# High and low weight tiles of 1032 columns, the last eight unused

## The chip, the cores and the metric

The kernel runs on one core of a Trainium2 chip. The metric is the device time of one execution, in microseconds. Before the change it is 2703.74 us, the median of three runs (2702.44 to 2708.98).

## What is computed

A two-layer backbone over 512 latent tokens and 256 context tokens of width 1024. Each layer is a half-step SwiGLU, a mixing stage with three groups of heads, and another half-step SwiGLU; shift, scale and gate come from a conditioning vector. All of it is in float32.

```python
for l in range(DEPTH):                                   # DEPTH = 2
    ml = jnp.split(s_lat @ w_mod[l] + b_mod[l], 9, axis=-1)
    mc = jnp.split(s_ctx @ w_mod[l] + b_mod[l], 9, axis=-1)
    x = half_ffn(x, g_norm[l, 0], ml[0], ml[1], ml[2], w_gate[l, 0], w_up[l, 0], w_down[l, 0])
    ctx = half_ffn(ctx, g_norm[l, 0], mc[0], mc[1], mc[2], w_gate[l, 0], w_up[l, 0], w_down[l, 0])
    h_lat = modulate(rms_norm(x, g_norm[l, 1]), ml[3], ml[4])
    h_ctx = modulate(rms_norm(ctx, g_norm[l, 1]), mc[3], mc[4])
    y_l, y_c = token_mixing(h_lat, h_ctx, w_in[l], w_out[l], ...)
    x = x + ml[5] * y_l
    x = half_ffn(x, g_norm[l, 2], ml[6], ml[7], ml[8], w_gate[l, 1], w_up[l, 1], w_down[l, 1])
    ...
# half_ffn: h + 0.5 * gate * ((silu(m @ wg) * (m @ wu)) @ wd),  m = modulate(rms_norm(h), shift, scale)
```

`half_ffn` has 2816 hidden columns, in 22 blocks of 128. The mixing stage is grouped-query attention, a short gated convolution and multi-head latent attention on one input projection, with one output projection behind them.

## The kernel before

Activations lie transposed, features on the 128 partitions and tokens along the row: `xT[0..7]` hold the stream, 128x768 each. A matrix product in float32 is made of three products in float32r: every operand is kept as a high part (the value rounded to float32r) and a low part (the remainder), and `mm3` (line 284) issues weight-high times data-high, weight-high times data-low and weight-low times data-high into one accumulator. So each 128x128 block of weights costs three matmuls per stretch of tokens, two with the high tile of the weights and one with the low tile, and each matmul loads its weights anew. In `PE MATMUL ps<-s,wh` of a profile, `s` is the moving operand (activations) and `wh` the weights.

Weights come in blocks of 128 rows by 1024 columns, which is eight 128x128 blocks. `wload` (line 194) fetches one into a raw tile `wr`. `wsplit` (line 199) makes the two parts: ScalarE copies `wr` to the high tile `wh`, and VectorE subtracts `wh` from `wr` into the low tile `wl`. Tiles `wh` and `wl` come from a pool with three buffers for each tag, so six buffers in all that are handed out in turn. Lines 554 and 873 take tiles of the same two tags, for a third early block and in the feed-forward of the last layer. In the mixing stage the tags also serve query and key tiles (`qh`, `ql`, `k`, 768 columns). Raw weights also come from other tiles: `wu` (tag `mscr`), `ws` (sums of weights, tag `mr`), `t` (down projections).

Most feed-forward blocks use a scheme of seven products on quarter matrices in place of eight; it needs sums of weights (`Weights.sums`, line 754, and `Sums` in the last layer, line 879) which go through the same split.

The order on TensorE, VectorE and ScalarE is written out by hand in most stages (`chain` and `behind` add an order without a semaphore). DMAs for weights are issued on SP's queue; some that add onto a tile come from GpSimd's. All vector, scalar and matrix instructions are recorded through one helper, so all of them have line 67 in the profile; tiles tell them apart.

SBUF addresses are given out by tag, one tag behind the other in the pool, each tag's buffers side by side.

Of the kernel before, what the change touches and what calls it, by code (L numbers as in the profile page):

```python
# [9 lines left out]
F32R = mybir.dt.float32r  # L10
# [5 lines left out]
P = 128  # L16
# [32 lines left out]
def tile_net(ctx: ExitStack, tc: tile.TileContext, a, out):  # L49
# [37 lines left out]
    pool = ctx.enter_context(tc.tile_pool(name="pool", bufs=1))  # L87
# [4 lines left out]
    def nm(s):  # L92
        uid[0] += 1
        return f"{s}{uid[0]}"
# [13 lines left out]
    def po():  # L108
        return psum.tile([P, 512], F32, name=nm("po"), tag="po", bufs=4)

    def f32(t):
        return t.bitcast(F32)
# [78 lines left out]
                mod_block(*mod_queue.pop(0))  # L191


    def wload(src, w):
        raw = pool.tile([P, 1024], F32, name=nm("wr"), tag="wr", bufs=NWR)
        nc.sync.dma_start(out=raw[:, :w], in_=src)
        return raw

    def wsplit(raw, w, hi=None, lo=None, eng=None):
        if hi is None:  # L200
            hi = pool.tile([P, 1024], F32R, name=nm("wh"), tag="wh", bufs=3)
            lo = pool.tile([P, 1024], F32R, name=nm("wl"), tag="wl", bufs=3)
        se.copy(hi[:, :w], raw[:, :w])
        (eng or ve).tensor_sub(lo[:, :w], raw[:, :w], f32(hi)[:, :w])
        return hi, lo
# [21 lines left out]
    def wblock(src, w=1024):  # L227
        return wsplit(wload(src, w), w)
# [89 lines left out]
    def rsqrt(ms, n, tag="rs", bufs=3):  # L318
        y, steps = rsqrt_steps(ms, n, tag, bufs)
        for f in steps:  # L320
            f()
        return y
# [96 lines left out]
    def lat_mm(acc, wb, h, k, cols, view):  # L419
        c = slice(k * P, (k + 1) * P)  # L420
        mm3(wb[0][:, c], wb[1][:, c], h[k][0], h[k][1], packed(acc, cols, view), k == 0, k == KD - 1)

    def residual(blocks, rhs, gate, streams, nxt, pre=None, late={}, view=nv, npump=0, ntail=3):
# [30 lines left out]
        if not two:  # L454
            return None
        held = [(o, blocks(o)) for o in range(KD - ntail, KD)]
        raws = [wload(src, 1024) for src in pre[:2]]
        E = []
        nk = len(rhs)

        def second_block():
            E.append(wsplit(raws[1], 1024, *(pool.tile([P, 1024], F32R, name=nm("we"), tag=t, bufs=1)
                                             for t in ("mscr", "mq"))))
            raws.append(wload(pre[2], 1024))

        chain("te", "ve", "se")
        for n, (o, wb) in enumerate(held):
            pt = po()
            project(packed(pt, c0, view), wb, rhs)
            update(o, cv(pt, c0), c0, i0)  # L470
            if n:
                S[0].accumulate()
            S[0].square(tv(xT[o], c0))
            if n == 1:
                E.append(wsplit(raws[0], 1024, *(pool.tile([P, 1024], F32R, name=nm("we"), tag="mr", bufs=2)
                                                 for _ in range(2))))
            elif n == 3:
                second_block()
# [5 lines left out]
        def run(count):  # L484
            for _ in range(count):
                if not units:
                    return
                n, k = units.pop(0)
                if k == 0:
                    if n % 2 == 0:  # L490
                        tiles[n // 2] = ps()
                project(packed(tiles[n // 2][:, BANK * (n % 2):BANK * (n % 2 + 1)], c1, view), held[n][1], rhs, [k])
                if k == nk - 1:
                    ready.append(n)
# [3 lines left out]
        def second_update():  # L498
            if ready:
                n = ready.pop(0)  # L500
                o = held[n][0]
                update(o, cv(tiles[n // 2][:, BANK * (n % 2):BANK * (n % 2 + 1)], c1), c1, i1)
                updated.append(o)

        def second_square():

            if updated:
                n = squared[0]
                squared[0] += 1
                if n % 3 == 0:  # L510
                    squared[1] = temp()
                w = S[1].w
                sq = squared[1][:, n % 3 * w:n % 3 * w + w]
                se.activation(out=cv(sq, c1), in_=tv(xT[updated.pop(0)], c1), func=AF.Square)
                s1.append(sq)
# [27 lines left out]
        def products(k):  # L543
            for n in range(len(accs)):
                lat_mm(accs[n], E[n], h, k, c0, hview)

        third = []
        for k in range(KD + 1):
            if k < KD:
                cur = HMod(h[k], k, c0, R, A[i0][:, k:k + 1], B[i0][:, k:k + 1], hview)  # L550
                cur.scaled()
                cur.high()
            if k == 4 and len(E) == 2:
                third.extend(pool.tile([P, 1024], F32R, name=nm(t), tag=t, bufs=3) for t in ("wh", "wl"))
                se.copy(third[0], raws[2])
            if prev is not None:
                prev.low()
            if k == 5 and third:
                ve.tensor_sub(third[1], raws[2], f32(third[0]))
                E.append(tuple(third))  # L560
            second_update()
            second_square()
            run(3)
            if k == 1:
                S[1].zero()
                S[1].count(S[1].acc, False)
            if k >= 1:
                for _ in range(2 if k < 6 else len(s1)):
                    if s1:
                        S[1].count(s1.pop(0), not (s1 or ready or updated or units))  # L570
            if k == 6:
                S[1].mean()
                r1 = rsqrt(S[1].ms, S[1].w // P)
            if prev is not None and (k <= hold or k == KD):
                products(k - 1)
            prev = cur
            if k == 7:

                R1 = po()
                for j in range(S[1].w // P):  # L580
                    te.transpose(out=R1[:, j * P:(j + 1) * P], in_=r1[:, j:j + 1].to_broadcast([P, P]), identity=ident)
                if len(accs) == 2:
                    accs.append(po())
                    for kk in range(hold):
                        lat_mm(accs[2], E[2], h, kk, c0, hview)
                for kk in range(hold, 7):
                    products(kk)
# [17 lines left out]
    def ffn(l, f, hin, streams, nxt, pre, npump, late={}):  # L605
# [111 lines left out]
        for ci in range(nslow):  # L717
            m0, n = chunks[ci]
            acts, ahead = [], {}
            for m in range(m0, m0 + n):  # L720
                if i == 0 and m > 1:
                    pump(2 - ci)
                acts.append(classical(m, ahead))
                if i == 0 and m < 2:
                    pump(2)
                if m in sums_at:
                    if m + 1 < m0 + n:
                        for j in range(2):
                            if 2 * (m + 1) + j >= len(E):
                                ahead[m + 1, j] = wblock(a[("wg", "wu")[j]][i, m + 1])  # L730
                    sums(sums_at.index(m))
            if ci == 0:
                pump(upto=gate)
            residual(down(m0, n), acts, gate, streams, None, view=view)
# [55 lines left out]
        lo, hi = slice(0, hw), slice(hw, w)  # L790
# [74 lines left out]
        def narrow():  # L865
# [4 lines left out]
            W = {}  # L870

            def high_part(raw, n=1024):
                hi = pool.tile([P, 1024], F32R, name=nm("wh"), tag="wh", bufs=3)
                lo = pool.tile([P, 1024], F32R, name=nm("wl"), tag="wl", bufs=3)
                se.copy(hi[:, :n], raw[:, :n])
                return (hi, lo), lambda: ve.tensor_sub(lo[:, :n], raw[:, :n], f32(hi)[:, :n])

            class Sums:
# [27 lines left out]
                def split_gate(self):  # L906
                    self.w1, low = high_part(self.g)
                    return low

                def split_sums(self):  # L910
                    self.w2, low = high_part(self.s)
                    return low

                def split_up(self):
                    self.w3, low = high_part(self.u)
                    return low
# [35 lines left out]
            for ci in range(1, len(LAST)):  # L952
                m0, n = LAST[ci]
                tiles = []
                for m in range(m0, m0 + n):
# [8 lines left out]
                    if j == 0:  # L964
                        t = nt
# [20 lines left out]
                    t = Tile(m, W[m])  # L986
# [153 lines left out]
        for ci in range(nslow, len(chunks)):  # L1140
# [3 lines left out]
            for m in range(m0, m0 + n):  # L1144
                end = m == m0 + n - 1
                nx = None
                if m == m0:

                    t = nt
# [23 lines left out]
                t = Tile(m)  # L1173
# [275 lines left out]
    def mixing(l, hin, early, streams, nxt, pre):  # L1449
# [513 lines left out]
        pump(upto=(l, 7))  # L1963
        pump(upto=(l, 6))
        return residual(lambda o: first_out[0] if o == 0 else wblock(a["wo"][l, o]), rhs, (l, 5), streams, nxt, pre, npump=2)

    def cst(name, l, shape):
# [276 lines left out]
```

## Time and profile before

| | |
|---|---|
| median of three runs | 2703.74 us |
| the profiled execution: its time | 2708.69 us |
| its span, first to last instruction | 2706.8 us |
| granted TensorE clock | 0.998 |
| matmuls | 16,088, TensorE busy 98% of the span |
| VectorE / ScalarE / GpSimd busy | 76% / 42% / 5% |
| DMA | 266.09 MB, 98 GB/s over the span |

Matmuls are pipelined, and the profile models their ends. The busy time of TensorE is a union of overlapping spans, so a matmul of 384 columns shows some 334 ns although the next one starts 173 ns later. The distance between starts, from the timeline, is what a matmul costs. A row of the timeline merges like instructions that follow each other: its start, the time they cover, and their count. PEld is the weight load, which runs beside the matmul before it. A row of the groups ends with the idle time of the engine just before these instructions and what ended it.

### The profile page before, as it was taken

What the parts mean: (1) busy time and instruction counts of PE and PEld (TensorE: products, weight loads), DVE (VectorE), ACT (ScalarE), POOL (GpSimd) and SP (SyncE); (2) the same over time, 40 slices, a digit from 0 to 9 for tenths busy, and PEclk for the clock granted to TensorE, in tenths of its full rate; (3) what the DMA queues carried; (4) which work ended last, traced back from release to release, by engine and by line L of the source; (5) the groups of instructions that cost most, each with busy time, mean ns of one, the idle gap of its engine ahead of it and who ended that gap; (6) DMA issues with size and microseconds to landing.
All of it is one profiled execution on the core that took longest, in us unless ns stands there. A gap on an engine that the chain in (4) does not pass through costs nothing. (4 is left out here: it accounts for less than half of the span.)

```text
span 2706.8 us, 40646 instructions
## 1 busy us (share of the span) xinstructions
PE 2647.6 (98%) x16088; PEld 2513.8 (93%) x16088; DVE 2047.0 (76%) x3493; ACT 1140.6 (42%) x1991; POOL 147.3 (5%) x224
## 2 busy tenths in 40 slices
PE   8999999999999999999999999999999999999999
PEld 5999999989888889999999999999998888889988
DVE  6856777777789987777777777777767798676655
ACT  5223333341478633333334433333343488444433
POOL 0000000000230100000000000000000221001110
PEclk9999999999999999999999999999999999999999
DMA  7313333234100321333333123333325101246544
GB/s 253 117 59 106 105 105 108 84 88 149 36 2 9 110 94 55 108 103 109 109 109 102 59 83 106 109 104 104 101 88 162 49 9 40 92 126 176 148 134 120
DMA packets 102927, 266.09 MB, mean 98 GB/s; under 512 B 12240, under 2 KB 41680, under 8 KB 102736
## 3 DMA queue, kind: packets, MB, share of 16 engines
q1 hardware_dynamic: 96112, 249.33, 27.8%
q0 software_dynamic: 6624, 14.16, 2.6%
q8 instruction: 127, 2.08, 0.3%
q14 instruction: 64, 0.52, 0.1%
HBM read 256.63 MB, written 2.10 MB: 96 GB/s over the span
## 5 line engine op out<-in xcount | busy, mean ns | idle before, releaser
L67 PE MATMUL ps<-s,wh 128*128 128x384 f32 (+2 forms) x4292 | 983.6, 338 | 7.5 <-ACT t L67 3.8
L67 PEld LDWEIGHTS ps<-s,wh 128*128 128x128 f32 x4292 | 742.5, 188 | 51.3 <-issue 5.2
L67 PE MATMUL po<-s,wh 128*128 128x384 f32 (+2 forms) x3164 | 765.2, 327 | 2.9 <-ACT t L67 2.2
L67 PE MATMUL ps<-s,wl 128*128 128x384 f32 (+2 forms) x2146 | 610.4, 337 | 1.3 <-DVE wl L67 1.2
L67 PEld LDWEIGHTS po<-s,wh 128*128 128x128 f32 x3164 | 554.4, 189 | 15.5 <-ACT t L67 3.3
L67 PE MATMUL po<-s,wl 128*128 128x384 f32 (+2 forms) x1582 | 517.2, 327 | 0.0
L67 PEld LDWEIGHTS ps<-s,wl 128*128 128x128 f32 x2146 | 387.3, 188 | 20.1 <-DVE wl L67 3.5
L67 PEld LDWEIGHTS po<-s,wl 128*128 128x128 f32 x1582 | 299.1, 189 | 5.4
L67 DVE SCALAR_TENSOR_TENSOR junk<-mr,sb 128x1024 fp8e4<-128x1024 f32 x224 | 273.7, 1222 | 16.1 <-DMA mr<-in_wm_dram 15.3
L67 DVE TENSOR_TENSOR wl<-wr,wh 128x1024 fp32r<-128x1024 f32 (+3 forms) x179 | 193.1, 1081 | 112.9 <-ACT wh L67 112.7
L67 DVE SCALAR_TENSOR_TENSOR xT<-ps,mod,xT 128x256 f32<-128x256 f32 (+1 forms) x360 | 198.7, 594 | 103.4 <-PE ps L67 101.3
L67 ACT CAST wh<-wr 128x1024 fp32r<-128x1024 f32 (+3 forms) x179 | 165.2, 926 | 202.9 <-PE ps L67 137.7
L67 ACT COPY t<-po 128x384 f32<-128x384 f32 (+2 forms) x215 | 96.9, 451 | 258.9 <-PE po L67 258.5
L67 PE MATMUL po<-s,s 128*128 128x256 f32 (+3 forms) x1216 | 191.9, 309 | 7.3 <-ACT s L67 2.7
L67 PEld LDWEIGHTS po<-s,s 128*128 128x128 f32 x1216 | 173.8, 191 | 14.8 <-ACT s L67 3.4
L67 ACT ACTIVATE t<-t 128x384 f32<-128x384 f32 (+1 forms) x142 | 70.9, 499 | 255.0 <-DVE t L67 255.0
L67 DVE TENSOR_TENSOR t<-po,t 128x384 f32<-128x384 f32 (+2 forms) x223 | 115.7, 524 | 34.2 <-ACT t L67 23.9
L67 DVE TENSOR_TENSOR s<-t,s 128x768 fp32r<-128x768 f32 (+3 forms) x144 | 104.2, 727 | 43.4 <-ACT s L67 42.9
L67 ACT CAST wh<-ws 128x1024 fp32r<-128x1024 f32 x71 | 74.6, 1051 | 147.0 <-PE ps L67 90.6
L67 ACT CAST s<-t 128x768 fp32r<-128x768 f32 (+3 forms) x144 | 92.6, 649 | 102.7 <-DVE t L67 102.5
L67 PE MATMUL po<-s,w 128*128 128x384 f32 x636 | 118.7, 334 | 0.0
L67 ACT CAST wh<-t 128x768 fp32r<-128x768 f32 x80 | 66.7, 837 | 113.6 <-PE ps L67 108.7
(197 smaller groups left out, 3306.7 us busy)
## 6 DMA issues: line engine op xcount, KB each, us to landing
mr<-in_wm_dram SPq DMA_DIRECT2D x128, 512.0 KB, 3.3
wr<-in_wg_dram SPq DMA_DIRECT2D x82, 512.0 KB, 3.3
wu<-in_wu_dram SPq DMA_DIRECT2D x71, 512.0 KB, 3.3
t<-in_wd_dram SPq DMA_DIRECT2D x80, 384.0 KB, 3.6
wr<-in_wiT_dram SPq DMA_DIRECT2D x22, 512.0 KB, 3.6
ws<-in_wu_dram POOLq DMA_DIRECT2D x36, 256.0 KB, 4.3
wr<-in_wu_dram SPq DMA_DIRECT2D x17, 512.0 KB, 3.3
wr<-in_wo_dram SPq DMA_DIRECT2D x14, 512.0 KB, 4.0
```

Of the source, the lines that this page charges most:

```text
L67: f(*args, **kw)
```

## The change

The high and low tiles become 1032 columns of four bytes, 4128 bytes instead of 4096, and a view of the first 1024 is handed on. Three places that made such tiles call one new function, `wtile`.

```diff
+    def wtile(tag):
+        return pool.tile([P, 1032], F32R, name=nm(tag), tag=tag, bufs=3)[:, :1024]
+
     def wsplit(raw, w, hi=None, lo=None, eng=None):
         if hi is None:
-            hi = pool.tile([P, 1024], F32R, name=nm("wh"), tag="wh", bufs=3)
-            lo = pool.tile([P, 1024], F32R, name=nm("wl"), tag="wl", bufs=3)
+            hi = wtile("wh")
+            lo = wtile("wl")
         se.copy(hi[:, :w], raw[:, :w])
         (eng or ve).tensor_sub(lo[:, :w], raw[:, :w], f32(hi)[:, :w])
         return hi, lo
...
             if k == 4 and len(E) == 2:
-                third.extend(pool.tile([P, 1024], F32R, name=nm(t), tag=t, bufs=3) for t in ("wh", "wl"))
+                third.extend(wtile(t) for t in ("wh", "wl"))
                 se.copy(third[0], raws[2])
...
             def high_part(raw, n=1024):
-                hi = pool.tile([P, 1024], F32R, name=nm("wh"), tag="wh", bufs=3)
-                lo = pool.tile([P, 1024], F32R, name=nm("wl"), tag="wl", bufs=3)
+                hi = wtile("wh")
+                lo = wtile("wl")
                 se.copy(hi[:, :n], raw[:, :n])
```

No instruction is added, taken away or moved on any engine; the instructions, their order and the semaphores they wait on are the same. What differs is where tiles lie. The built program gives these byte addresses within a partition:

| buffer | before | rest by 128 | after | rest by 128 | rest by 256 |
|---|---|---|---|---|---|
| `wh`, first | 189248 | 64 | 189248 | 64 | 64 |
| `wh`, second | 193344 | 64 | 193376 | 96 | 96 |
| `wh`, third | 197440 | 64 | 197504 | 0 | 128 |
| `wl`, first | 201536 | 64 | 201632 | 32 | 160 |
| `wl`, second | 205632 | 64 | 205760 | 64 | 192 |
| `wl`, third | 209728 | 64 | 209888 | 96 | 224 |
| `mr`, first | 213824 | 64 | 214016 | 0 | 0 |
| `mr`, second | 217920 | 64 | 218112 | 0 | 0 |
| `mq` | 222016 | 64 | 222208 | 0 | 0 |
| `s` (34 slots), `t` (5), `wr` (2), `mscr` | 54080 to 189247 | 64 | as before | 64 | 64 |
| `xT` (8) | 17120 to 41695 | 96 | as before | 96 | 224, 224, ... |

Blocks of 128 columns within a tile start 512 bytes apart, so every block has its tile's rest.

## Prediction

> **What bounds the kernel now.** I read the page's parts 1, 2 and 4 first, then the list of waits of TensorE alone, then the groups of instructions with shapes kept apart, and last the timeline at places where nothing is waited for.
>
> ```profile
> span 2706.8 us, 40646 instructions
> PE 2647.6 (98%) x16088; PEld 2513.8 (93%) x16088; DVE 2047.0 (76%) x3493; ACT 1140.6 (42%) x1991; POOL 147.3 (5%) x224
> PEclk9999999999999999999999999999999999999999
> PE 17%; DVE 2%; ACT 1%; issue 1%; DMA 0%; POOL 0%; ACTq 0%; DVEq 0%; POOLq 0%
> ```
>
> TensorE has work in 98% of the span, its granted clock is full throughout, and in the chain that ended last no other engine has over 2%. The waits of TensorE (who it waited for: us in total, times, longest) confirm it; these four are the largest, and no row of that list names a DMA:
>
> ```profile
> PE po L67 <- ACT t L67: 8.9, 18, 1.1
> PE po L67 <- DVE s L67: 8.3, 10, 4.5
> PE ps L67 <- ACT t L67: 8.3, 11, 1.6
> PE ps L67 <- DVE s L67: 3.3, 5, 1.8
> ...
> PE ps L67 <- DVE wl L67: 1.2, 4, 0.5
> ...
> PE ps L67 <- ACT wh L67: 0.2, 1, 0.2
> ```
>
> The last two are the waits for the tiles of this change: 1.4 us in all. So the time is the spacing of 16,088 matmuls, and the question is whether an address can change that spacing. These groups take their weights from `wh` and `wl` (out<-moving,weights; count | busy, mean ns of one; a matmul's own ns overlaps its neighbours'):
>
> ```profile
> L67 PE MATMUL ps<-s,wh 128*128 128x384 f32 (+2 forms) x4292 | 983.6, 338 | 7.5 <-ACT t L67 3.8
> L67 PE MATMUL po<-s,wh 128*128 128x384 f32 (+2 forms) x3164 | 765.2, 327 | 2.9 <-ACT t L67 2.2
> L67 PE MATMUL ps<-s,wl 128*128 128x384 f32 (+2 forms) x2146 | 610.4, 337 | 1.3 <-DVE wl L67 1.2
> L67 PE MATMUL po<-s,wl 128*128 128x384 f32 (+2 forms) x1582 | 517.2, 327 | 0.0
> ...
> L67 PE MATMUL ps<-s,wh 128*128 128x384 f32 x2720 | 600.7, 335 | 4.1 <-ACT t L67 1.9 <-DVE xT L67 1.0
> L67 PE MATMUL po<-s,wh 128*128 128x384 f32 x2120 | 537.9, 334 | 1.7 <-ACT t L67 1.7
> ...
> L67 PE MATMUL ps<-s,wh 128*128 128x256 f32 x740 | 161.6, 284 | 1.6 <-ACT t L67 0.9 <-DVE xT L67 0.4 <-DVE s L67 0.2
> L67 PE MATMUL po<-s,wh 128*128 128x256 f32 x768 | 141.5, 285 | 0.5 <-ACT t L67 0.5
> ```
>
> The first four are part 5 of the page, the others the same groups with shapes kept apart. In all there are 4292+3164+2146+1582 = 11,184. Each product runs as two matmuls with `wh` and one with `wl`, so a width counts one and a half times its `wh` rows: 384 columns (2720+2120)·1.5 = 7,260 times, 256 columns (740+768)·1.5 = 2,262 times, and 1,662 are left for 512 columns.
>
> The true spacing is read from starts in the timeline (start us, length us, engine, names, shapes, count), one stretch for each width:
>
> ```profile
> 111.81 0.85 PE L67 MATMUL ps<-s,wh 128*128 128x384 f32 x4
> ...
> 114.94 0.85 PE L67 MATMUL ps<-s,wh 128*128 128x384 f32 x4
> ...
> 2001.16 0.62 PE L67 MATMUL po<-s,wh 128*128 128x512 f32 x2
> ...
> 2003.21 0.62 PE L67 MATMUL po<-s,wh 128*128 128x512 f32 x2
> ...
> 2440.53 0.40 PE L67 MATMUL po<-s,wh 128*128 128x256 f32 x2
> ...
> 2441.61 0.40 PE L67 MATMUL po<-s,wh 128*128 128x256 f32 x2
> ```
>
> Between the first pair lie 18 matmuls (three rounds of four with `wh` and two with `wl`): 3.13/18 = 174 ns. Between the second pair 9: 2.05/9 = 228 ns (227 over longer stretches). Between the third 9: 1.08/9 = 120 ns. From 256 to 512 columns the spacing grows by 107 ns, so a column costs 0.417 ns and **13.3 ns are fixed** in every matmul (120 − 256·0.417). The 11,184 matmuls take 7260·0.1735 + 1662·0.227 + 2262·0.120 = 1,908 us, 70% of the span; their fixed part is 149 us. That fixed part is the only thing on the path on which an address could act.
>
> **What the change does to the instructions.** On all five engines the instructions, their order and their waits are the same before and after; only addresses differ. So the work in count is zero added, zero removed, nothing moved, and the sum is over what each access costs at its new address. Four kinds touch the moved tiles.
>
> *Weight loads and matmuls.* Before, all six buffers and all moving tiles (`s`) start 64 bytes past a multiple of 128. After, the six start at 64, 96, 128, 160, 192 and 224 bytes past a multiple of 256: six offsets indeed, but against a period of 128 bytes two of them equal the old one, and three are now odd multiples of 32. Is the fixed 13.3 ns a collision of the weight read with the moving read? The trace has matmuls with nearly no weights to read: the modulation products at the start, whose weights are 4 columns wide, and lie in 16-byte steps.
>
> ```profile
> 31.85 2.04 PE L67 MATMUL ps<-s,s 128*4 128x256 f32 x16
> ...
> L67 PEld LDWEIGHTS ps<-s,s 128*4 128x4 f32 x96 | 7.5, 84 | 4.2 <-DVE s L67 1.2 <-ACT s L67 0.2
> L67 PE MATMUL ps<-s,s 128*4 128x256 f32 x96 | 12.5, 279 | 0.9 <-DVE s L67 0.7
> ...
> L67 PEld LDWEIGHTS ps<-s,wh 128*128 128x128 f32 x4292 | 742.5, 188 | 51.3 <-issue 5.2 <-ACT t L67 4.9 <-ACT s L67 2.3
> ```
>
> Sixteen of them in 2.04 us: (2.04 − 0.28)/15 = 117.3 ns each, against 120 with 128 columns of weights. With 1/32 of the weight data gone, 10.6 of the 13.3 ns stay. So at most 2.7 ns of a matmul can be a collision with its weight read, and four of six buffers get a new offset against 128, taken as two thirds of the 11,184, or 7,456: 2.7 · 7,456 = 20 us is the most that I grant to the gain. In the other direction: a load of 128 columns takes 188 ns, one of 4 takes 84, so a column takes 0.84 ns and the transfer of a whole load 107 ns. That fits under a spacing of 120, 174 or 227 ns with 13, 66 or 120 ns to spare. A load that got longer at an odd multiple of 32 bytes costs nothing until it grew by 13 ns. I take **0** for both.
>
> [...]
>
> *ScalarE's copies into `wh` and VectorE's subtractions into `wl`.* The tiles `xT` lie at an odd multiple of 32 bytes already (96 past a multiple of 128), beside `s` at 64:
>
> ```profile
> L67 DVE SCALAR_TENSOR_TENSOR s<-t,mod,s 128x512 fp32r<-128x512 f32 x32 | 23.9, 747 | 0.5
> L67 DVE SCALAR_TENSOR_TENSOR t<-xT,mod,po 128x512 f32<-128x512 f32 x32 | 23.7, 741 | 0.2
> L67 DVE SCALAR_TENSOR_TENSOR xT<-po,mod,xT 128x512 f32<-128x512 f32 x21 | 15.7, 748 | 8.8 <-PE po L67 8.8
> ...
> L67 DVE TENSOR_TENSOR wl<-wr,wh 128x1024 fp32r<-128x1024 f32 x129 | 159.4, 1238 | 102.8 <-ACT wh L67 102.7
> ...
> L67 DVE TENSOR_TENSOR wl<-wr,wh 128x512 fp32r<-128x512 f32 x16 | 10.9, 683 | 0.0
> ```
>
> 741 to 748 ns wherever the operands lie: reading or writing at 32 past a multiple of 64 is free on VectorE. The subtraction into `wl` reads two tiles and writes a third, all three at the same offset today, at (1238 − 683)/512 = 1.08 ns an element; by the spread of the `xT` rows (7 of 748) a new offset moves it by 1% at most. Neither reaches the path: VectorE has 24% idle, and TensorE waits 1.4 us in all for `wl` and `wh`. I take 0, with 1.4 us as the gain's end and the 129 longest at 12 ns, 1.5 us, as the loss's.
>
> *Matmuls that stream from these buffers, and the tiles laid behind them.* Three groups stream `wh`, `wl` or the keys `k`; two tags behind (`mr`, `mq`) move by 192 bytes to multiples of 256, and DMAs fill most of them or add onto them:
>
> ```profile
> L67 PEld LDWEIGHTS ps<-k,s 128*128 128x128 f32 x162 | 28.6, 189 | 10.1 <-ACT t L67 4.4 <-issue 2.0 <-PE po L67 0.6
> L67 PEld LDWEIGHTS ps<-wh,s 128*128 128x128 f32 x156 | 27.8, 188 | 2.7 <-issue 2.7
> L67 PEld LDWEIGHTS ps<-wl,s 128*128 128x128 f32 x78 | 14.7, 188 | 0.0
> ...
> wg<-ws POOLq DMA_DIRECT2D x6, 256.0 KB, 5.9
> ```
>
> The streams are at most 162 + 156 + 78 = 396 matmuls; bounded by the whole fixed part, 13.3 ns either way, 5 us. The slowest of the DMAs lands in 5.9 us, six times; 5% either way is 0.3 us each, and no wait of TensorE names a DMA, so at most 2 us. I take 0 for both.
>
> **The sum** is 0 on the profiled execution: span 2706.8, its own time 2708.7 us. That execution lies 5 us over the median of the runs shown, 2703.74 (2702.44 to 2708.98), so I predict **2703.7 us**. About 0.3% (8 us) is what a measurement of this kernel can tell from no change.
>
> **The rivals.** (1) *The fixed part is a collision after all, and goes where the offset differs.* For it: every `s` and every weight buffer shares the offset of 64, so the trace has no full-width weight load at another. Against it: the 4-column rows. Granted in full, 13.3 · 7,456 = 99 us, 2605 us; bounded by those rows, 20 us, 2684 us. [...] Chance 0.06 for a gain over 0.3%.
>
> (2) *Slower: a weight load at an odd multiple of 32 bytes reads more pieces.* Three of six buffers, half of the matmuls. It decides from 13 ns of growth (107 to 120), in the 256-column form first. At a quarter more (27 ns) 1,131 matmuls pay 14 ns: 16 us, 2720. At twice as long (107 more) they pay 94 ns, and 3,630 of 384 columns pay 41: 106 + 149 = 255 us, 2959. For it: no full load at such an address is in the trace. Against it: VectorE's rows on `xT` only. Chance 0.05.
>
> (3) *The change doesn't do what it says*: if only the offset against 128 counts, it makes four offsets, not six; the time is the forecast's either way.
>
> **How the numbers follow.** No change 0.89, rival 1 0.06, rival 2 0.05. The range 2695 to 2712 is no change with 0.3% to either side, which holds 0.89; reaching for 2684 or 2720 would add little.
>
> **What would show it.** Right: the spacings of 174, 227 and 120 ns, the weight load's 188 ns, VectorE's 1,238 and the `xT` rows all stand again. Rival 1: the 384-column spacing falls towards 160 in products with some buffers and not with others. Rival 2: the load's 188 ns grows and the 256-column form spreads first. I am wrong if any spacing moves by over 1 ns: 1 ns on 11,184 matmuls is 11 us.

## The result, and the profile after

The changed kernel takes 2721.73 us (median of four runs, 2719.02 to 2727.01) beside 2704.74 us before (four runs): a ratio of 1.0063, with a 95% interval of 1.0043 to 1.0084. It is slower by 17 us, where no change was forecast, and 9.7 us above the range.

The page of the changed kernel, parts 1, 2 and 5:

```profile
span 2725.2 us, 40646 instructions
PE 2667.1 (98%) x16088; PEld 2527.1 (93%) x16088; DVE 2046.6 (75%) x3493; ACT 1141.0 (42%) x1991; POOL 146.7 (5%) x224
PEclk9999999999999999999999999999999999999999
...
L67 PE MATMUL ps<-s,wh 128*128 128x384 f32 (+2 forms) x4292 | 991.6, 340 | 7.3 <-ACT t L67 3.8
L67 PEld LDWEIGHTS ps<-s,wh 128*128 128x128 f32 x4292 | 743.7, 188 | 52.1 <-ACT t L67 4.9
```

The span grew by 18.4 us and the busy time of TensorE by 19.5, with the same instructions; VectorE and ScalarE are busy as long as before, to 0.4 us. So the loss is in the matmuls. The weight load still takes 188 ns. The other rows that the prediction looked at stand as well: TensorE's waits for the moved tiles, then VectorE's shapes:

```profile
PE ps L67 <- DVE wl L67: 1.0, 4, 0.3
...
PE ps L67 <- ACT wh L67: 0.5, 1, 0.5
...
L67 DVE TENSOR_TENSOR wl<-wr,wh 128x1024 fp32r<-128x1024 f32 x129 | 159.2, 1236 | 102.5 <-ACT wh L67 102.3
L67 DVE SCALAR_TENSOR_TENSOR xT<-po,mod,xT 128x512 f32<-128x512 f32 x21 | 15.7, 747 | 8.9 <-PE po L67 8.9
```

The spacing of the matmuls is best seen in the chain of work that ended last, in order of time (start us, length us, what, count). In the last feed-forward block it has pieces of 108 matmuls of 512 columns and of 72 of 256 columns in which nothing else stands. Before:

```profile
2490.19 24.51 PE ps L67 x108
2524.77 8.64 PE po L67 x72
```

After:

```profile
2505.47 25.06 PE ps L67 x108
2540.52 8.56 PE po L67 x72
```

At 512 columns the spacing went from 24.51/108 = 226.9 to 232.0 ns; at 256 columns from 120.0 to 118.9. For 384 columns I count matmuls in 105 us of the first feed-forward block, where TensorE never pauses (busy time by stretch; us, TensorE's busy time and count, clock, DMA share and rate). Before, then after:

```profile
90.00:195.00 105.00, 105.00 (x607) 1.00 0.29 92
...
90.00:195.00 105.00, 105.00 (x602) 1.00 0.28 90
```

Five matmuls fewer in the same time, at the same clock: about 0.8% more per matmul, or 1.4 ns.

Since the program is the same, the start-to-start distances of the two traces can be compared matmul by matmul. In all they grow by 18.3 us, but not all of that comes from addresses. Besides their last 2 us, each of these two traces has stretches of 3 to 10 us in which the granted clock is half, at different places: in the traced execution after the change at 581 us (for 6.8 us) and 735 us (10.2), in the one before at 657 and 2353 us (3.4 each). The same piece of the program before, at the full clock, and after, at half (timeline rows, then the clock of that stretch):

```profile
578.93 0.95 PE L67 MATMUL ps<-ones,t 128*128 128x2 f32 x8
579.74 1.65 PE L67 MATMUL po<-s,we 128*128 128x512 f32 x6
```

```profile
583.18 1.70 PE L67 MATMUL ps<-ones,t 128*128 128x2 f32 x8
584.74 2.91 PE L67 MATMUL po<-s,we 128*128 128x512 f32 x6
...
583.00:587.00 4.00, 4.00 (x14) 0.50 0.02 4
```

The matmuls with `ones`, which no tile of the change touches, slow down there as much as the others. These stretches make 7.0 us of the execution after and 5.0 us of the one before, so 2.0 us of the difference. Outside them, the 384-column matmuls with weights from the six buffers make 11.2 us, those of 512 columns 4.9 us, and those of 256 columns nothing (0.03 us). A further 0.6 us comes from the 192 matmuls of 512 columns that take weights from `we` tiles (high part in `mscr` and low part in `mq`, or both in `mr`).

### The profile page after: what moved, and what is told of

Read it like the earlier page. It is cut to its first block, busy times and chain, and to the rows that moved or that the text cites. A ratio compares the mean times of both kernels' runs of the same rounds, so it can differ in the third digit from the quotient of the medians.

```text
span 2725.2 us, 40646 instructions
## 1 busy us (share of the span) xinstructions
PE 2667.1 (98%) x16088; PEld 2527.1 (93%) x16088; DVE 2046.6 (75%) x3493; ACT 1141.0 (42%) x1991; POOL 146.7 (5%) x224
## 5 line engine op out<-in xcount | busy, mean ns | idle before, releaser
L67 PEld LDWEIGHTS po<-s,wh 128*128 128x128 f32 x3164 | 554.3, 188 | 18.4 <-ACT t L67 5.4
L67 PE MATMUL po<-s,w 128*128 128x384 f32 x636 | 118.9, 336 | 0.0
```

The lines of the kernel that those rows point to most:

```text
L67: f(*args, **kw)
```

## The experiments

None of these kernels adds, removes or moves an instruction. Pads (tiles that nothing uses) shift the tiles that come behind them. Addresses are told by their rest; the distance is from the moving tile's rest to that of the weights. The theories named in the expectations are: **D**, high and low weights of one product at different rests cost; **O**, an odd multiple of 32 bytes costs by itself (rival 2 of the prediction); **M**, weights off the moving tile's rest cost; **B**, the tiles behind are the cause; and, from the second set on, **R**, only differences between addresses count. The result given for each is the ratio to the kernel before with its 95% interval.

**First set: which buffers are off from what.** The edit, with the three pads in bytes:

```diff
     def wtile(tag):
-        return pool.tile([P, 1032], F32R, name=nm(tag), tag=tag, bufs=3)[:, :1024]
+        first = tag not in made
+        made.add(tag)
+        if first:
+            pad("x" + tag, HIGH if tag == "wh" else LOW)
+        t = pool.tile([P, COLS], F32R, name=nm(tag), tag=tag, bufs=3)[:, :1024]
+        if first and tag == "wl":
+            pad("xend", END)
+        return t
```

All six buffers 32 bytes on (HIGH 32, LOW 0, END 224, 1024 columns):

> All six buffers at 96 (mod 128), moving tiles at 64, tiles behind at 64 again; tiles of 1024 columns. Theory D (high and low weights of one product at different rests is what costs): high and low agree, so no change against before: 2704 us, ratio 1.000, 384-column spacing 173.4 ns. Rival O (weights at an odd multiple of 32 bytes cost by themselves): six of six buffers odd against three of six in the change, so twice the change's loss: ratio 1.012. Rival M (weights off the moving tile's rest cost): six of six off against four of six: ratio 1.009. Rival B (the tiles behind, moved by 192 bytes, are the cause): ratio 1.000.

Measured 1.0013 (1.0000 to 1.0026). O and M fall in this form: all six buffers are odd and off the moving tile, and almost nothing is lost. D is right on the total and on 384 columns (x608 in the same 105 us), but not on 512 columns:

```profile
2495.67 25.19 PE ps L67 x108
2530.83 8.53 PE po L67 x72
```

High and low agree here, and the 512-column spacing is still 233.2 ns. So distance from the moving tile counts too, in that width.

Low buffers 64 on (LOW 64, END 192), nothing odd:

> High buffers at 64, low buffers at 0 (mod 128), tiles behind at 64 again; nothing at an odd multiple of 32. Theory D: as slow as the change, ratio 1.006, 384-column spacing 175 ns, 512-column spacing 231. Rival O: 1.000. Rival M: only the low third of the matmuls is off, ratio 1.003. Rival B: 1.000.

Measured 1.0040 (1.0021 to 1.0059): O and B fall, since no weight tile lies at an odd multiple of 32 and the tiles behind have their rest back.

Low buffers 32 on (LOW 32, END 224):

> High buffers at 64, low buffers at 96 (mod 128), tiles behind at 64 again. Theory D: as the change, ratio 1.006. Rival O: the low third of the matmuls odd, against half in the change: ratio 1.004. Rival M: 1.003. Rival B: 1.000.

Measured 1.0108 (1.0092 to 1.0123), more than any theory gave. The same stretches show it:

```profile
90.00:195.00 105.00, 105.00 (x592) 1.00 0.29 91
...
2514.39 25.20 PE ps L67 x108
```

592 matmuls in place of 607, although only one load in three has moved. With all six at 32 the count was 608. At 384 columns the difference between high and low is what costs here: either distance alone was free.

Pairs that agree mod 128 (LOW 32, END 32, 1032 columns):

> Tiles of 1032 columns as in the change, but high and low buffer of the same number agree (mod 128): 64 and 64, 96 and 96, 0 and 0; tiles behind at 64 again. Theory D with a period of 128 bytes: ratio 1.000; with a period of 256 or more the pairs differ by 128 and it is 1.006. Rival O: two of six odd: ratio 1.004. Rival M: four of six off the moving rest, as in the change: ratio 1.006. Rival B: 1.000.

Measured 1.0047 (1.0033 to 1.0062). The pairs agree mod 128 and differ by 128 mod 256, and they are slow: D with a period of 128 falls. A distance of 128 by itself is in the third set.

**Second set: differences alone?** One pad of 32 bytes ahead of the pool, so that moving tiles and weights shift together:

> One pad of 32 bytes ahead of the whole pool: moving tiles, raw tiles, all six buffers and the tiles behind lie at 352 (mod 512) instead of 320, all at an odd multiple of 32. Theory R (only the differences between addresses count: low against high buffer, and weights against the moving tile, by their rest mod 512): no change against before, ratio 1.000, spacings 120, 173.4 and 227 ns again. Rival O (an odd multiple of 32 bytes costs by itself): ratio over 1.006.

Measured 0.9992 (0.9981 to 1.0003), and the spacings are those of before to the last digit, with all of these operands at odd multiples of 32:

```profile
90.00:195.00 105.00, 105.00 (x607) 1.00 0.29 92
...
2485.36 24.51 PE ps L67 x108
2519.95 8.64 PE po L67 x72
```

O is refuted; R holds. All six 64 on (HIGH 64, END 192):

> All six buffers at 384 (mod 512), 64 past the moving tile's 320, tiles behind at 64. Theory R: like the run with all six at 352: high and low agree, so 384 columns at 173.4 ns; weights off the moving tile, so 512 columns at 231 to 233 ns, 256 columns 1 to 2 ns below before; ratio 1.001. Rival O: 1.000 in every width, since nothing is odd.

Measured 1.0054 (1.0038 to 1.0070), a miss for R as I had put it: high and low agree, and the products of two highs and a low still run at 175.3 ns a matmul at 384 columns. Agreement isn't enough; the distance of 64 costs in that width too.

Only the tiles behind moved (END 192, 1024 columns, buffers as before the change):

> Buffers as before the change, only the tiles behind them (mr, mq) at 0 (mod 512) as in the change. Theory R: only the matmuls that take weights from these tiles can move, above all the 192 of 512 columns whose high part lies in mscr and low part in mq, by some 10 ns: 2 us, ratio 1.001. Rival B (the tiles behind are the cause of the change's loss): ratio 1.006.

Measured 1.0013 (1.0000 to 1.0026): the tiles behind are not the cause. Matmul by matmul the same 192 lose 0.6 us outside the stretches at half clock, as in the change.

Pairs that agree mod 512, at distances 0, 32 and 64. Six small tiles of constants are laid between the tags in place of a pad:

> Tiles of 1032 columns as in the change, but six small tiles of constants are laid between the tags, so that high and low buffer of a number agree mod 512 (320, 352, 384). Theory R: 384 columns back at 173.4 ns for all three pairs; 512 columns 227 for the first pair and 231 to 233 for the others; ratio 1.001 to 1.002. Rival O: one pair of three odd: ratio 1.004. Rival M (weights off the moving tile cost in every width): 384 columns at 175 for the second and third pair, ratio 1.006.

Measured 1.0038 (1.0027 to 1.0050). At 384 columns the pairs stand at 173.9, 173.4 and 175.4 ns, at 512 columns at 228.0, 233.1 and 233.3: each pair within 0.7 ns of the whole kernel at its distance. The ratio is over the 1.002 expected, because the pair at 64 costs at 384 columns too.

**Third set: the distance by itself.** The kernel before, with one line added ahead of the first weight tile (`Rs`, line 2079), so that `mscr`, `wr`, the six buffers, `mr` and `mq` shift alike:

```diff
+    pool.tile([P, BYTES // 4], F32, name="pad", tag="pad", bufs=1)
     Rs = pool.tile([P, D], F32, name="Rs", tag="mscr", bufs=1)
```

> The kernel before with one pad of 256 bytes ahead of every weight tile (mscr, wr, wh, wl, mr, mq), so that all weights lie 256 past the moving tile's rest mod 512, high and low alike. Only the distance from the weights to the moving tile differs. If the spacing repeats with a period of 256 bytes or less: ratio 1.000 and 120, 173.4, 227 ns. If the period is 512: any other spacing, 512 columns at 231 to 233 as at distances 32 and 64, ratio 1.001 to 1.006. If distance did not count and only high against low did: 1.000 here and in the next three runs.

> The same with a pad of 128 bytes. A period of 128 gives 1.000; since a pair 128 apart was slow, I expect 512 columns at 231 to 233 ns and a ratio of 1.002 to 1.006.

> The same with a pad of 192 bytes. The 384-column matmuls with weights in mr stood at this distance in the change and at 173.3 ns, so 384 columns 173.3 for all; 512 columns unknown, 227 to 233; ratio 0.999 to 1.003.

> The same with a pad of 96 bytes. The matmuls with weights in mr stood at this distance in the run with agreeing pairs, at 173.7 ns for 384 columns; 512 columns 231 to 233 as at 32 and 64; 256 columns below 118; ratio 1.000 to 1.004.

> A pad of 224 bytes ahead of every weight tile: the last but one of the eight distances in steps of 32 within the period of 256. At 192 the 384-column form stood at 173.3 ns, 256 columns at 115.2 and 512 columns at 229.0; at 256 (and 0) they stood at 173.4, 119.9 and 227.3. If the spacing changes steadily between: 173.3, 117 and 228 ns, 5 us under before, ratio 0.998 to 0.999. If each distance is on its own: 384 columns at 173 or 175, ratio 0.998 to 1.006.

> The same with a pad of 160 bytes. 384 columns stood at 175.8 at 128 and at 173.3 at 192: either of them here; 512 columns between 232.6 and 229; 256 columns 115 to 119. At 384 columns of 173.3 the ratio is 1.000 to 1.002, at 175.8 1.004 to 1.007.

A distance of 256 gives the kernel before again (1.0002; 24.51 and 8.64 us in the chain, x608 in the stretch) and 128 doesn't (1.0081, x599), so the period, as far as tried, is 256 bytes; distances other than 0 were not tried a second time 256 bytes on. The distances of 128 and 160 cost more than expected. All of it, as mean spacing in ns over all products of two highs and a low with nothing waited for between; the last columns are the time that these spacings give on 7,260, 1,662 and 2,262 matmuls, and the time measured (ratio less one, times 2,708 us):

| run | distance | 256 columns | 384 | 512 | by spacings, us | measured, us | ratio, interval |
|---|---|---|---|---|---|---|---|
| before | 0 | 119.9 | 173.4 | 227.3 | 0 | 0 | 1 |
| pool moved by 32 | 0 | 119.9 | 173.4 | 227.4 | 0 | -2 | 0.9992 (0.9981 to 1.0003) |
| all six by 32 | 32 | 118.3 | 173.4 | 233.3 | 6 | 4 | 1.0013 (1.0000 to 1.0026) |
| all six by 64 | 64 | 116.9 | 175.3 | 233.3 | 17 | 15 | 1.0054 (1.0038 to 1.0070) |
| pad of 96 | 96 | 117.6 | 173.3 | 234.1 | 6 | 1 | 1.0003 (0.9994 to 1.0013) |
| pad of 128 | 128 | 118.7 | 175.8 | 232.6 | 24 | 22 | 1.0081 (1.0063 to 1.0098) |
| pad of 160 | 160 | 119.8 | 176.7 | 233.3 | 33 | 31 | 1.0113 (1.0098 to 1.0128) |
| pad of 192 | 192 | 115.2 | 173.3 | 229.0 | -8 | 0 | 1.0000 (0.9985 to 1.0014) |
| pad of 224 | 224 | 116.9 | 173.5 | 233.3 | 4 | 8 | 1.0030 (1.0015 to 1.0045) |
| pad of 256 | 256 | 119.9 | 173.4 | 227.3 | 0 | 1 | 1.0002 (0.9989 to 1.0015) |
| low by 64 | 0 and 64 | 117.9 | 174.8 | 231.2 | 12 | 11 | 1.0040 (1.0021 to 1.0059) |
| low by 32 | 0 and 32 | 118.5 | 176.7 | 233.2 | 30 | 29 | 1.0108 (1.0092 to 1.0123) |

The spacing of three widths accounts for every run to within 8 us, the large losses to within 3. It is rough, since it gives all matmuls of a width the spacing of the products of two highs and a low. Summed matmul by matmul outside half-clock stretches, the three widths at 192 make -7.0 - 0.2 + 2.8 = -4 us in place of -8. The two extremes, in the rows of their chains and stretches, at 160:

```profile
2456.28 8.63 PE po L67 x72
...
2515.55 25.21 PE ps L67 x108
...
90.00:195.00 105.00, 105.00 (x596) 1.00 0.29 91
```

and at 192:

```profile
2446.97 8.24 PE po L67 x72
...
2485.70 24.73 PE ps L67 x108
...
90.00:195.00 105.00, 105.00 (x608) 1.00 0.29 93
```

At 192, 256 columns take 114.4 ns in this piece instead of 120.0, 384 columns are as before and 512 columns lose 2 ns. It is the only distance whose sum of spacings is under before, but its ratio is 1.0000: no version was found that measurably beats the kernel before. The expectation of a steady change between 192 and 256 failed at 224, where 512 columns stand at 233.3 ns.

## Why the prediction was wrong

- **What bounds the kernel**, the spacing of the matmuls, was right: outside the stretches at half clock, the matmuls that take weights from moved tiles lose 16.8 us, and all others together gain 0.5. (The clock is not quite "full throughout" in the execution before: 3.4 us at 657 us and 3.4 us at 2353 us are at half, too short to show in forty slices.) That an address could act on a fixed part alone was not. The spacing of 256 columns fell by 1.1 ns in the chain's pieces and that of 512 rose by 5.1, which is no constant added to every matmul.
- **The step that failed** is the one on weight loads and matmuls: "at most 2.7 ns of a matmul can be a collision with its weight read" and, for the loss, "costs nothing until it grew by 13 ns". The 4-column products (117.3 ns beside 120) say how little would be saved by reading fewer weights at the distances that they had. They say nothing of what a full load costs at a distance from the moving tile that the trace did not hold. There the spacing moves both ways, from -4.7 ns (256 columns at 192) to +6.8 (512 columns at 96), which is over the 2.7 ns granted. At 192 the 256-column matmuls with full weights run at 114.4 ns in their piece, under the 117.3 of the 4-column ones, so those rows were no floor.
- **The change's own spacings.** Its pairs stand at distances 0 and 96, 32 and 128, 64 and 160. At 384 columns they run at 175.6, 174.9 and 175.2 ns, at 512 columns at 232.3, 231.3 and 232.1, and at 256 columns at 118.8, 119.6 and 118.6. On even thirds that makes 1.8 · 7,260 + 4.6 · 1,662 - 0.9 · 2,262 = 19 us; 17 were measured. The prediction put this term at 0.
- **Rival 2**, slower from odd multiples of 32 bytes, had a time of 2720 near the measured 2722, but not for the reason it gave. The load kept its 188 ns; the 256-column form, said to lose first, lost nothing (119.0 ns on average over the change's pairs, 119.9 before); 512 columns, with 120 ns to spare, lost most per matmul (4.6 ns); the run with all of these operands at odd multiples was as fast as before (0.9992).
- **Rival 1** had it right that the spacing depends on the distance (227.3 to 234.1 ns at 512 columns) and wrong that another distance takes the fixed 13.3 ns away: the largest gain is 4.7 ns, at 256 columns and 192. The kernel before already stood at the best distance for 384 and 512 columns of the eight tried, or within 0.1 ns of it.
- **Rival 3** asked whether six offsets are only four against a period of 128. The runs show 256 as the period, as far as tried (1.0002 at 256, 1.0081 at 128), so that all six differ; the loss doesn't follow from that count, but from the distances.
- **VectorE, ScalarE and the waits**: as predicted, 1,236 ns for 1,238, 747 for 748, 1.5 us of waits for 1.4. **The matmuls that stream from the moved tiles** were taken at 0, and outside half-clock stretches they changed by 0.1 us in all. **The tiles behind** were taken at 0 on the ground that no wait names a DMA; as weights of matmuls they cost 0.6 us.
- **An address has an effect of its own**: with the same two streams the spacing of 512 columns is 227.3 ns at a distance of 0 and 233.3 at 32, 64, 160 and 224.

What stays open is the mechanism. The spacing depends on the distance and on the width, and on whether high and low differ (0 and 32 are each free at 384 columns, together they cost 3.3 ns). It also depends on the place in the kernel. In the long stretch of the first feed-forward block, where four highs and two lows follow each other, 384 columns take 173.3 ns at a distance of 64 and 176.7 at 224 (x607 and x596 in the 105 us), while the products of two highs and a low take 175.3 and 173.5. Later products of four highs and two lows take 176.9 at 64 and 174.9 at 224, against 174.1 before, so the order alone doesn't decide it. No run here shows why.

## What to carry to other kernels

Where float32r matmuls of 384 or 512 columns follow each other without a pause, as here, keep the weight tiles, high and low, and the moving tiles at one rest mod 256 bytes; a pad that broke this cost from nothing (1.0000 at 192) to 1.1% (1.0113 at 160), though no matmul's mean spacing rose by more than 6.8 ns. At 256 columns no distance tried was slower than 0 (115.2 to 119.9 ns, 119.9 at 0), so a kernel of that width alone may choose otherwise. A trace in which all operands share a rest cannot bound what another rest costs: here the fixed 13.3 ns stood over the largest gain, 4.7 ns, but nothing in the trace before told of a loss of 6.8 ns. Before laying out tiles at spread offsets, compare the counts of matmuls in one stretch without waits, and look at the granted clock of that stretch first: 7 us at half clock made 192 matmuls look 2.2 us slower, of which 0.6 was the address.

## What the runs showed of the hardware that was not expected

- The spacing of back-to-back float32r matmuls depended on the distance between the weights' and the moving tile's address: 227.3 to 234.1 ns at 512 columns, 173.3 to 176.7 at 384, 115.2 to 119.9 at 256. A distance of 256 bytes gave the three spacings of 0 again (227.3, 173.4 and 119.9 ns). Moving both alike by 32 changed nothing (0.9992; 227.4, 173.4 and 119.9 ns).
- The distance that was worst for one width was neutral for another: 160 cost 3.3 ns at 384 columns (176.7 beside 173.4) and nothing at 256 (119.8 beside 119.9).
- The duration of the loads from `wh` and `wl`, 188 to 189 ns in every run, shows none of it.
- In the middle of a busy span the granted clock was half for 3 to 10 us, at places that differ between executions of the same instructions: at 581 and 735 us after the change, at 657 and 2353 us before it, nowhere between 20 and 2700 us in the run with a pad of 96, whose mean granted clock is 1.000. No run here shows what sets it off.
